# Reordering the steps of windowed attention in a two-layer decoder on one core

## The chip, the core and the metric

The kernel runs on one core of a Trainium2 chip. The metric is device time in microseconds (us) from launch to the last output; the lower the better. The core has five engines that run their own instruction streams and wait for each other through semaphores: TensorE (PE, matmuls; its weight loads are shown as PEld), VectorE (DVE), ScalarE (ACT), GpSimd (POOL) and SyncE (SP, which here only starts DMA transfers).

## The reference

A decoder trunk of two layers over 512 tokens with a model width of 1024, in float32. Layer 0 is a gated position mixer, a gated MLP with a short convolution, and a gated embedding. After it one shared key/value projection is made. Layer 1 is windowed attention over those keys and values, then the same MLP and embedding. The change is in the attention, whose core is:

```python
q = (xn @ w_q).reshape(B, nb, BLOCK, N_KV_HEADS, GQA_GROUP, HEAD_DIM)      # 4 blocks of 128, 4 groups of 4 heads
scores = jnp.einsum('bnikgd,bnjkd->bnkgij', q, kblk) * (HEAD_DIM ** -0.5)  # keys: previous and current block
scores = scores - slopes[:, :, None, None] * dist                          # ALiBi
scores = jnp.where(valid, scores, -jnp.inf)                                # window of 128, causal
m = jnp.maximum(jnp.max(scores, axis=-1, keepdims=True), sink)
e = jnp.exp(scores - m)
probs = e / (jnp.sum(e, axis=-1, keepdims=True) + jnp.exp(sink - m))
out = jnp.einsum('bnkgij,bnjkd->bnikgd', probs, vblk)
return out.reshape(B, S, N_Q_HEADS * HEAD_DIM) @ w_o
```

## The kernel before

**Products.** Every large product is made from float32 operands that are split in two parts, a high one (`wh`, `oh`, `n11h`, ...) and a low one (`wl`, `ol`, `n11l`, ...): three matmuls of 128 x 512 for each 128 rows of contraction (`mm3`, lines 212 to 214). Weights arrive by DMA in units of 512 KB (`wraw`, `load`); `pump` splits a unit, the high part on ACT (L185), the low part on DVE (L186). PE is in use for nearly the whole time.

**Attention in 16 steps.** A step is a pair of a key/value group g and a block n of 128 queries, g outer. For step i these pieces exist:

- `scores(i)` (L731): eight matmuls on PE into the tile `sc`, of which one buffer exists.
- `logits(i)` (L744, L745, L747, L750): DVE selects the window, scales and adds the ALiBi term, and takes the minimum `low` (the logits carry a minus sign). In a step with n = 0 L747 stands in L744's place, behind L745.
- `exps(i)` (L758): four exponentials on ACT, one for each head, each followed by a read-out of its sum into `sm`.
- `inverse(i)` (L763): the reciprocal of the four sums on DVE. `weights(i)` (L768): their product with the exponentials on POOL, in the tile `prs`.
- `turn(i)` (L775): four transposes on PE into `tr`. `turned_hi(i)` (L790, ACT) and `turned_lo(i)` (L795, DVE) split them into a high and a low part (`ph` and `pl` or `pp`), and `masks(i)` (L802, POOL) makes the masked copies `pm` for the difference of two value blocks.
- `mix(i)` (L816): the value product, four matmuls (two in a step with n = 0) into `pv`, of which one buffer exists. `low_rows(i)` (L822, ACT) copies its lower half to `pb`; `outputs(i)` adds the halves in two instructions on DVE (L834), after which `pv` is free, and makes the high part `oh` on ACT (L838); `output_lows(i)` makes the low part `ol` on POOL (L844).

**What runs beside it.** PE would be idle while a step goes through the other engines. So each step also has five entries of the list `work` (seven in the first), each of three matmuls: 48 entries for the queries of the later groups (`project`), then entries of the output projection (`merge`, tiles `o4`, `o5`, ...). `fill(i, a, b)` emits a step's entries a to b. When a query tile is complete, `queries` splits it (high part L274 on ACT, low part L275 on DVE) and sends the parts to their places by four DMAs; when an output tile is complete, DVE adds it to `h` (L865). Both are put in `held` and emitted by `settle()`.

**What sets the order.** Inside the block `in_order(...)` the order in which the code calls these pieces is the order on PE, DVE, ACT and POOL: each instruction follows the one before it on its engine. The loop of a step calls, in this order (step i >= 3):

```python
o = scores(i); weights(i - 1)
pairs = outputs(i - 3, *done.pop(i - 3)); logits(i, o); output_lows(pairs, nc.gpsimd)
pump(...); fill(i, 0, 3); tr = turn(i - 1); sinks(i + 1)
exps(i, (0, 1)); turned_hi(i - 1, tr); exps(i, (2, 3)); masks(...); turned_lo(i - 1, tr)
fill(i, 3, 4); settle(); pv = mix(i - 2); fill(i, 4, None)
inverse(i); done[i - 2] = pv, low_rows(i - 2, pv)
```

So a block's two sums (L834) are made one step after its value product, ahead of the next step's logits; the reciprocal stands at the end of the step, behind a query tile's split; and POOL's product of the probabilities opens the following step.

Of the kernel before, what the change touches and what calls it, by code (L numbers as in the profile page):

```python
# [52 lines left out]
def tile_yoco(ctx: ExitStack, tc: tile.TileContext, t, out: bass.AP, out_b: bass.AP):  # L53
    nc = tc.nc
# [36 lines left out]
    units = []  # L91
# [63 lines left out]
    def load(upto, queue=nc.sync):  # L155
        while state["raw"] < min(upto, len(units)):
            j = state["raw"]
            a, m, _ = units[j]
            tags = state["tags"]
            r = wp.tile([P, UNIT], F32, tag=f"r{tags[state['turn'] % len(tags)]}", bufs=1, name=f"wraw{j}")  # L160
            state["turn"] += 1
            if len(a.shape) == 4:
                for c in range(2):
                    queue.dma_start(r[:, :m].rearrange("p (k c n) -> p k c n", c=2, n=256)[:, :, c], a[:, :, c])
            else:
                queue.dma_start(r[:, :m], a)
            raws[j] = r
            state["raw"] += 1

    def pump(upto):  # L170
        while state["unit"] < min(upto, state["cap"]):
            u = state["unit"]
            _, n, own = units[u]
            load(u + 1)
            if own:
                pool, *tags = own
                wh, wl = (pool.tile([P, n], F32R, tag=tg, name=f"own{u}_{tg}") for tg in tags)
            else:
                wh = wp.tile([P, UNIT], F32R, tag="wh", bufs=WBUFS, name=f"wh{u}")
                wl = wp.tile([P, UNIT], F32R, tag="wl", bufs=WBUFS, name=f"wl{u}")  # L180
            src = raws.pop(u)[:, :n]
            if u == 0:
                nc.vector.tensor_copy(wh[:, :n], src)
            else:
                nc.scalar.copy(wh[:, :n], src)  # L185
            nc.vector.tensor_sub(wl[:, :n], src, wh[:, :n].bitcast(F32))  # L186
            ready[u] = (wh, wl, n)
            state["unit"] += 1
# [565 lines left out]
    def exps(i, es):  # L754

        pr, low, sm = live[i]
        for e in es:
            nc.scalar.activation(pr[:, e, :], pr[:, e, :], AF.Exp, bias=low[:, e : e + 1], scale=-1.0,  # L758
                                 accum_out=sm[:, e : e + 1])

    def inverse(i):

        nc.vector.reciprocal(live[i][2], live[i][2])  # L763

    def weights(i):

        pr, low, sm = live[i]
        nc.gpsimd.tensor_mul(pr[:, :, :P], pr[:, :, :P], sm.unsqueeze(2).to_broadcast([P, GQ, P]))  # L768
# [36 lines left out]
    def mix(i):  # L805

        g, n = steps[i]
        ph, pl, mh, ml = live.pop(i)
        cur = vt[n // 2][:, n % 2, g, :]
        terms = [(cur, ph), (cur, pl)]  # L810
        if n:
            dif = vd[:, n - 1, g, :]
            terms = [(cur, ph), (dif, mh), (cur, pl), (dif, ml)]
        ps = psum(f"pv{i}", "pv")
        for a, (lhs, rhs) in enumerate(terms):
            nc.tensor.matmul(ps, lhs, rhs, start=a == 0, stop=a == len(terms) - 1)  # L816
        return ps

    def low_rows(i, ps):

        b = tp.tile([P, S], F32, tag="rstd", name=f"pb{i}")
        nc.scalar.copy(b[:HD, :], ps[HD:, :])  # L822
        return b

    def outputs(i, ps, b):

        g, n = steps[i]
        if n == 0:
            for m in (2 * g, 2 * g + 1):
                o2.append([ap.tile([P, S], F32R, tag=f"a{x}{m}", name=f"o{x}{m}") for x in "hl"])  # L830
        x, y = (a.rearrange("p (b e t) -> p b e t", b=2, e=2) for a in (ps, b))
        of = y[:, :, 0, :]
        for e in range(2):
            nc.vector.tensor_add(of[sides[e]], x[:HD, :, e, :], y[:HD, :, e, :])  # L834
        cols = slice(n * P, (n + 1) * P)
        pairs = [(of[:, a, :], *(x[:, cols] for x in o2[2 * g + a])) for a in range(2)]
        for src, oh, ol in pairs:
            nc.scalar.copy(oh, src)  # L838
        return pairs

    def output_lows(pairs, eng):

        for src, oh, ol in pairs:
            eng.tensor_sub(ol, src, oh.bitcast(F32))  # L844
# [2 lines left out]
    held = []  # L847
    work = [(project, u) for u in range(48)]
    part = lambda m, k: (merge, m, k, k + 1, k == 0, k == 3 and m > 3)
    work += [part(m, k) for m, k in ((4, 0), (4, 1), (5, 0), (5, 1), (4, 2), (4, 3), (5, 2), (5, 3))]  # L850
    work += [part(m, k) for m in (6, 7, 0, 1, 2, 3) for k in range(4)]
    work += [part(0, 4), part(1, 4)]
    beside = [work[:7]] + [work[5 * i + 2 : 5 * i + 7] for i in range(1, last)]
    assert 5 * last + 2 == len(work)
# [2 lines left out]
    def fill(i, a, b):  # L857

        for f, *args in beside[i][a:b]:
            f(*args)  # L860

    def settle():

        for f, *args in held:
            f(*args)  # L865
        held.clear()
# [5 lines left out]
    with in_order(*engines):  # L872
        for i in range(last):
            o = scores(i)
            if i >= 1:
                weights(i - 1)
            if i >= 3:
                pairs = outputs(i - 3, *done.pop(i - 3))
            logits(i, o)
            if i >= 3:  # L880
                output_lows(pairs, nc.gpsimd)
            if i == 0:
                values(3)
            if i in pumped:
                pump(state["unit"] + 1)
            fill(i, 0, 3)
            if i:
                tr = turn(i - 1)
            if i + 1 < last:
                sinks(i + 1)  # L890
            exps(i, (0, 1))
            if i:
                turned_hi(i - 1, tr)
            exps(i, (2, 3))
            if i:
                masks(i - 1, (0,))
                turned_lo(i - 1, tr)
                masks(i - 1, (1,))
            fill(i, 3, 4)
            settle()  # L900
            if i >= 2:
                pv = mix(i - 2)
            fill(i, 4, None)
            inverse(i)
            if i % NC == NC - 1 and i + 1 < last:
                nc.vector.tensor_scalar_mul(alibi, alibi, slope(GQ - 1))
            if i >= 2:
                done[i - 2] = pv, low_rows(i - 2, pv)
            load(min(state["unit"] + 2, held_back))
        settle()  # L910
        weights(last - 1)
        output_lows(outputs(last - 3, *done.pop(last - 3)), nc.gpsimd)
        for m in (0, 1):
            merge(m, 5, 6, False, False)
        pv = mix(last - 2)
        done[last - 2] = pv, low_rows(last - 2, pv)
        merge(2, 4, 6, False, False)
        tr = turn(last - 1)
        turned_hi(last - 1, tr)
        masks(last - 1, (0,))  # L920
        turned_lo(last - 1, tr)
        masks(last - 1, (1,))
        output_lows(outputs(last - 2, *done.pop(last - 2)), nc.gpsimd)
    two = psum2("o4")
    merge(3, 4, 6, False, False)
    merge(4, 4, 6, True, False, two[:, 0])
# [219 lines left out]
```

## Time and profile before

| what | value |
|---|---|
| time, median of 3 runs | 1150.45 us (1149.15 to 1151.38) |
| the profiled execution, its own time | 1150.4 us |
| its span, first to last instruction | 1148.7 us |
| PE busy / DVE busy / ACT busy / POOL busy | 1125.6 / 734.6 / 509.8 / 136.0 us |
| mean granted TensorE clock | 0.996 |
| attention's 16 steps, first scores to last value product | from 590.8 us to about 703 us |

Busy time counts an instruction's whole duration; a matmul of 128 x 512 is shown with 389 ns, while the next one starts some 230 ns later, since they are pipelined. So an idle time of PE in the profile begins when the last matmul has ended by that model, and the distance between two starts is the better measure of what a wait costs.

### The profile page before, as it was taken

How to read it: one execution, taken by the hardware profiler on the slowest of the kernel's cores; microseconds unless marked ns; L12 is line 12 of the kernel's file. 1: busy time of each engine (PE TensorE's matmuls, PEld its weight loads, DVE VectorE, ACT ScalarE, POOL GpSimd, SP SyncE). 2: the span in 40 equal slices, each digit the busy share in tenths (PEclk: the TensorE clock that was granted, in tenths of full speed). 3: DMA queues.
4: the chain of work that ended last, by engine and by line, in shares of the span. 5: the costliest groups of instructions: out<-in, count | busy, mean ns of one | idle time of the engine just before them, and what ended most of it. 6: DMA issues, size and time to landing. Idle time of an engine off the chain costs nothing.

```text
span 1148.7 us, 13690 instructions
## 1 busy us (share of the span) xinstructions
PE 1125.6 (98%) x5248; PEld 938.3 (82%) x5248; DVE 734.6 (64%) x983; ACT 509.8 (44%) x808; POOL 136.0 (12%) x169
## 2 busy tenths in 40 slices
PE   9999999999999999999999899999999999999996
PEld 7888888888888888888897687888888888888895
DVE  7356477763676367557867776687735774577656
ACT  6534344431343244445646666554422442344532
POOL 2100310000000000022224444200000000000232
PEclk9999999999999999999999999999999999999998
DMA  9322222322322333233053314433323323332202
GB/s 319 123 80 86 98 94 91 110 94 90 110 82 83 110 113 99 83 110 110 19 147 110 110 56 147 147 110 92 110 82 102 95 71 110 110 97 85 79 15 74
DMA packets 44690, 116.48 MB, mean 101 GB/s; under 512 B 4936, under 2 KB 16848, under 8 KB 44624
## 3 DMA queue, kind: packets, MB, share of 16 engines
q1 hardware_dynamic: 43504, 114.42, 31.3%
q10 hardware_dynamic: 1120, 1.18, 0.3%
q8 instruction: 41, 0.67, 0.2%
q14 instruction: 25, 0.20, 0.1%
HBM read 108.24 MB, written 2.11 MB: 96 GB/s over the span
## 4 chain that ended last, share of the span: by engine, by line
PE 88%; DVE 5%; ACT 3%; issue 1%; POOL 1%; DMA 0%; SPq 0%; POOLq 0%; DVEq 0%; ACTq 0%
PE up L212 14%; PE up L213 14%; PE up L214 14%; PE d L212 8%; PE d L213 8%; PE d L214 8%; PE gate L212 2%; PE gate L213 2%; PE gate L214 2%; ACT prs L758 2%; PE u L214 1%; PE u L212 1%; PE u L213 1%; PE v L224 1%; PE v L223 1%; PE v L225 1%
## 5 line engine op out<-in xcount | busy, mean ns | idle before, releaser
L186 DVE TENSOR_TENSOR wl<-wraw,wh 128x1024 fp32r<-128x1024 f32 (+2 forms) x197 | 237.2, 1205 | 123.5 <-ACT wh L185 122.8
L185 ACT CAST wh<-wraw 128x1024 fp32r<-128x1024 f32 (+1 forms) x196 | 202.1, 1032 | 233.3 <-PE d L213 135.8
L212 PE MATMUL up<-nf00h,wh 128*128 128x512 f32 x352 | 137.1, 390 | 0.0
L212 PE MATMUL up<-nf10h,wh 128*128 128x512 f32 x352 | 137.0, 389 | 0.0
L214 PE MATMUL up<-nf00h,wl 128*128 128x512 f32 x352 | 137.0, 389 | 0.0
L214 PE MATMUL up<-nf10h,wl 128*128 128x512 f32 x352 | 136.9, 389 | 0.0
L213 PE MATMUL up<-nf00l,wh 128*128 128x512 f32 x352 | 136.9, 389 | 0.0
L212 PE MATMUL d<-ah,wh 128*128 128x512 f32 x352 | 136.9, 389 | 0.0
L213 PE MATMUL d<-al,wh 128*128 128x512 f32 x352 | 136.9, 389 | 0.0
L214 PE MATMUL d<-ah,wl 128*128 128x512 f32 x352 | 136.9, 389 | 0.0
L213 PE MATMUL up<-nf10l,wh 128*128 128x512 f32 x352 | 136.9, 389 | 0.0
L399 ACT ACTIVATE c<-hs,vec 128x512 f32<-128x512 f32 x88 | 71.7, 815 | 89.0 <-DVE hs L395 88.0
L400 DVE SCALAR_TENSOR_TENSOR c<-hs,vec,c 128x511 f32<-128x511 f32 x88 | 65.9, 749 | 37.4 <-ACT c L399 37.2
L373 DVE TENSOR_TENSOR h<-h,d 128x512 f32<-128x512 f32 x56 | 38.4, 686 | 69.0 <-PE d L214 69.0
L274 ACT CAST ah<-a 128x512 fp32r<-128x512 f32 x44 | 27.4, 622 | 113.5 <-DVE a L405 113.5
L214 PEld LDWEIGHTS up<-nf00h,wl 128*128 128x128 f32 x352 | 66.1, 188 | 13.8
L212 PEld LDWEIGHTS up<-nf10h,wh 128*128 128x128 f32 x352 | 66.1, 188 | 13.8
L214 PEld LDWEIGHTS d<-ah,wl 128*128 128x128 f32 x352 | 66.1, 188 | 13.8
L212 PEld LDWEIGHTS d<-ah,wh 128*128 128x128 f32 x352 | 66.1, 188 | 13.7
L213 PEld LDWEIGHTS up<-nf10l,wh 128*128 128x128 f32 x352 | 66.1, 188 | 13.7
L213 PEld LDWEIGHTS d<-al,wh 128*128 128x128 f32 x352 | 66.1, 188 | 13.6
L213 PEld LDWEIGHTS up<-nf00l,wh 128*128 128x128 f32 x352 | 66.1, 188 | 13.6
(316 smaller groups left out, 2028.6 us busy)
## 6 DMA issues: line engine op xcount, KB each, us to landing
wraw<-in_w_up SPq DMA_DIRECT2D x88, 512.0 KB, 3.5
wraw<-in_w_down SPq DMA_DIRECT2D x32, 512.0 KB, 3.6
wraw<-in_w_down SPq DMA_DIRECT2D x16, 384.0 KB, 3.2
wraw<-in_w_u SPq DMA_DIRECT2D x8, 512.0 KB, 6.7
wraw<-in_w_out SPq DMA_DIRECT2D x8, 512.0 KB, 3.5
wraw<-in_w_gate SPq DMA_DIRECT2D x8, 512.0 KB, 3.6
wraw<-in_w_q SPq DMA_DIRECT2D x8, 512.0 KB, 3.5
wraw<-in_w_o SPq DMA_DIRECT2D x8, 512.0 KB, 3.4
```

Of the source, the lines that this page charges most:

```text
L185: nc.scalar.copy(wh[:, :n], src)
L186: nc.vector.tensor_sub(wl[:, :n], src, wh[:, :n].bitcast(F32))
L212: nc.tensor.matmul(ps, wh[:, a:b], xh, start=st, stop=False)
L213: nc.tensor.matmul(ps, wh[:, a:b], xl, start=False, stop=False)
L214: nc.tensor.matmul(ps, wl[:, a:b], xh, start=False, stop=en)
L223: nc.tensor.matmul(ps, xh[:, s], wh[:, a:b], start=st, stop=False)
L224: nc.tensor.matmul(ps, xl[:, s], wh[:, a:b], start=False, stop=False)
L274: nc.scalar.copy(hi, src)
L373: nc.vector.tensor_add(h[m], h[m], ps)
L399: nc.scalar.activation(c, hs, AF.Identity, bias=v("conv_b", l * 2 * NJ + col), scale=cw[2])
L400: nc.vector.scalar_tensor_tensor(c[:, 1:], hs[:, : S - 1], cw[1], c[:, 1:], op0=ALU.mult, op1=ALU.add)
L758: nc.scalar.activation(pr[:, e, :], pr[:, e, :], AF.Exp, bias=low[:, e : e + 1], scale=-1.0, accum_out=sm[:, e : e + 1])
```

## The change

The number and kind of the instructions stay the same on every engine. The change puts attention's pieces in another order:

- `mix(i - 2)` moves from the step's end to right behind `scores(i)`, followed by its `low_rows`.
- `outputs(i - 2)`, with the two sums on DVE, is made in the same step, behind the logits' minimum, the first exponential and the low part of the turned probabilities. Before, it was made at the head of the next step.
- `inverse(i)` follows right behind these sums, ahead of the query tiles' splits and the additions to `h` of `settle()`, and POOL's `weights(i)` follows it in the same step.
- One exponential stands ahead of `turned_hi` on ACT instead of two; one entry of work stands ahead of the transposes on PE instead of three, three follow them, and the fifth closes the step.
- `pump` is cut in two, so that a unit's high part (ACT) stands ahead of the step's exponentials and its low part (DVE) behind them.
- The list of work puts the first two entries of output tile 6 ahead of the last two of tiles 4 and 5.

```diff
-    def pump(upto):
-        while state["unit"] < min(upto, state["cap"]):
-            u = state["unit"]
-            _, n, own = units[u]
-            load(u + 1)
+    half_done = {}
+
+    def pump_hi(u):
+
+        _, n, own = units[u]
+        load(u + 1)
+        if u not in half_done:
             if own:
...
                 nc.scalar.copy(wh[:, :n], src)
+            half_done[u] = wh, wl, n, src
+        return True
+
+    def pump(upto):
+        while state["unit"] < min(upto, state["cap"]):
+            u = state["unit"]
+            pump_hi(u)
+            wh, wl, n, src = half_done.pop(u)
             nc.vector.tensor_sub(wl[:, :n], src, wh[:, :n].bitcast(F32))
...
-    work += [part(m, k) for m, k in ((4, 0), (4, 1), (5, 0), (5, 1), (4, 2), (4, 3), (5, 2), (5, 3))]
-    work += [part(m, k) for m in (6, 7, 0, 1, 2, 3) for k in range(4)]
+    work += [part(m, k) for m, k in ((4, 0), (4, 1), (5, 0), (5, 1), (6, 0), (6, 1), (4, 2), (4, 3),
+                                             (5, 2), (5, 3), (6, 2), (6, 3))]
+    work += [part(m, k) for m in (7, 0, 1, 2, 3) for k in range(4)]
...
             o = scores(i)
-            if i >= 1:
-                weights(i - 1)
-            if i >= 3:
-                pairs = outputs(i - 3, *done.pop(i - 3))
             logits(i, o)
-            if i >= 3:
-                output_lows(pairs, nc.gpsimd)
+            cast = i and i in pumped and pump_hi(state["unit"])
+            if i >= 2:
+                pv = mix(i - 2)
+                low = low_rows(i - 2, pv)
             if i == 0:
                 values(3)
-            if i in pumped:
-                pump(state["unit"] + 1)
-            fill(i, 0, 3)
+            fill(i, 0, 1)
             if i:
                 tr = turn(i - 1)
             if i + 1 < last:
                 sinks(i + 1)
-            exps(i, (0, 1))
+            exps(i, (0,))
             if i:
                 turned_hi(i - 1, tr)
-            exps(i, (2, 3))
+            exps(i, (1, 2, 3))
+            if cast:
+                pump(state["unit"] + 1)
             if i:
                 masks(i - 1, (0,))
                 turned_lo(i - 1, tr)
                 masks(i - 1, (1,))
-            fill(i, 3, 4)
-            settle()
             if i >= 2:
-                pv = mix(i - 2)
-            fill(i, 4, None)
+                pairs = outputs(i - 2, pv, low)
             inverse(i)
+            weights(i)
+            if i >= 2:
+                output_lows(pairs, nc.gpsimd)
             if i % NC == NC - 1 and i + 1 < last:
                 nc.vector.tensor_scalar_mul(alibi, alibi, slope(GQ - 1))
-            if i >= 2:
-                done[i - 2] = pv, low_rows(i - 2, pv)
+            fill(i, 1, 4)
+            settle()
+            if i == 0:
+                pump(state["unit"] + 1)
+            fill(i, 4, None)
             load(min(state["unit"] + 2, held_back))
         settle()
-        weights(last - 1)
-        output_lows(outputs(last - 3, *done.pop(last - 3)), nc.gpsimd)
+        pv = mix(last - 2)
+        low = low_rows(last - 2, pv)
         for m in (0, 1):
             merge(m, 5, 6, False, False)
-        pv = mix(last - 2)
-        done[last - 2] = pv, low_rows(last - 2, pv)
+        pairs = outputs(last - 2, pv, low)
         merge(2, 4, 6, False, False)
         tr = turn(last - 1)
...
-        output_lows(outputs(last - 2, *done.pop(last - 2)), nc.gpsimd)
+        output_lows(pairs, nc.gpsimd)
```

**VectorE, from the logits of step 2 to the logits of step 3.** Names end in the step's number and a buffer number; `ql1_1` is the low part of a query tile, `pp1` that of the turned probabilities of step 1. Before:

```order
L750 TENSOR_REDUCE low2_4764<-prs_4587 128x4
L795 TENSOR_TENSOR pp1_4784<-tr1_4776,pp1_4784 128x512
L275 TENSOR_TENSOR ql1_1_4796<-q1_1_4712,qh1_1_4795 128x512
L763 RECIPROCAL sm2_4766<-sm2_4766 128x4
L834 TENSOR_TENSOR pb0_4813<-pv0_4805,pb0_4813 64x2x128 x2
L744 COPY_PREDICATED sc3_4815<-above_467,sc3_4815 128x4x128
L745 SCALAR_TENSOR_TENSOR prs_4587<-sc3_4815,rq_4382,alibi_4491 128x4x128
```

and with the change:

```order
L760 TENSOR_REDUCE low2_4764<-prs_4587 128x4
L805 TENSOR_TENSOR pp1_4782<-tr1_4775,pp1_4782 128x512
L844 TENSOR_TENSOR pb0_4770<-pv0_4767,pb0_4770 64x2x128 x2
L773 RECIPROCAL sm2_4766<-sm2_4766 128x4
L285 TENSOR_TENSOR ql1_1_4813<-q1_1_4728,qh1_1_4812 128x512
L754 COPY_PREDICATED sc3_4826<-above_467,sc3_4826 128x4x128
L755 SCALAR_TENSOR_TENSOR prs_4587<-sc3_4826,rq_4382,alibi_4491 128x4x128
```

The two sums and the reciprocal have moved ahead of the query tile's low part, which now stands alone between them and the next logits.

**TensorE, around the transposes of step 8 and the value product of step 7.** `o5_0` and `q3_1` are work that runs beside attention. Before, within step 9 and up to the scores of step 10:

```order
L775 MATMUL tr8_5275<-ident_131,prs_4587 128x128 x4
L212 MATMUL o5_0_5289<-oh0_4825,wh116_5043 128x512
L213 MATMUL o5_0_5289<-ol0_4826,wh116_5043 128x512
L214 MATMUL o5_0_5289<-oh0_4825,wl116_5044 128x512
L816 MATMUL pv7_5303<-pp7_5218,vt1_4489 128x512
L816 MATMUL pv7_5303<-pm7_5219,vd_4490 128x512
L816 MATMUL pv7_5303<-pp7_5218,vt1_4489 128x512
L816 MATMUL pv7_5303<-pm7_5219,vd_4490 128x512
L212 MATMUL o5_0_5289<-oh1_4827,wh116_5043 128x512
L213 MATMUL o5_0_5289<-ol1_4828,wh116_5043 128x512
L214 MATMUL o5_0_5289<-oh1_4827,wl116_5044 128x512
L731 MATMUL sc10_5316<-kh1_4288,q2_0_0_4945 128x256
```

and with the change, from the last scores of step 9:

```order
L741 MATMUL sc9_5247<-kl1_4290,q2_1_1_5100 128x256
L826 MATMUL pv7_5264<-pp7_5218,vt1_4489 128x512
L826 MATMUL pv7_5264<-pm7_5219,vd_4490 128x512
L826 MATMUL pv7_5264<-pp7_5218,vt1_4489 128x512
L826 MATMUL pv7_5264<-pm7_5219,vd_4490 128x512
L222 MATMUL q3_1_5168<-n11h7_3928,wh115_4908 128x512
L223 MATMUL q3_1_5168<-n11l7_3929,wh115_4908 128x512
L224 MATMUL q3_1_5168<-n11h7_3928,wl115_4909 128x512
L785 MATMUL tr8_5274<-ident_131,prs_4587 128x128 x4
```

The value product has moved ahead of the transposes, to the place behind the scores, with one entry of work between the two.

**TensorE, behind the scores of step 10.** `oh2` and `oh3` are outputs of the second group of heads, whose last block is step 7; `oh0` and `oh1` are of the first group. Before:

```order
L731 MATMUL sc10_5316<-kl1_4290,q2_1_1_5083 128x256
L212 MATMUL o4_0_5268<-oh2_5107,wh116_5043 128x512
L213 MATMUL o4_0_5268<-ol2_5108,wh116_5043 128x512
L214 MATMUL o4_0_5268<-oh2_5107,wl116_5044 128x512
L212 MATMUL o4_0_5268<-oh3_5109,wh116_5043 128x512
```

and with the change:

```order
L741 MATMUL sc10_5323<-kl1_4290,q2_1_1_5100 128x256
L826 MATMUL pv8_5340<-ph8_5281,vt0_4488 128x512
L826 MATMUL pv8_5340<-pl8_5282,vt0_4488 128x512
L222 MATMUL o6_0_5345<-oh0_4791,wh117_5122 128x512
L223 MATMUL o6_0_5345<-ol0_4792,wh117_5122 128x512
L224 MATMUL o6_0_5345<-oh0_4791,wl117_5123 128x512
L785 MATMUL tr9_5349<-ident_131,prs_4587 128x128 x4
L222 MATMUL o6_0_5345<-oh1_4793,wh117_5122 128x512
L223 MATMUL o6_0_5345<-ol1_4794,wh117_5122 128x512
L224 MATMUL o6_0_5345<-oh1_4793,wl117_5123 128x512
L222 MATMUL o4_0_5297<-oh2_5072,wh116_5043 128x512
```

The first matmul that reads the second group's outputs was the first one behind the scores; now it stands three items later, and those outputs are made one step earlier.

## The prediction

> **What bounds the kernel now.** I read the page's first rows, then PE's waits, then the granted clock around the longest wait, then the timelines of the engines there.
>
> ```profile
> span 1148.7 us, 13690 instructions
> PE 1125.6 (98%) x5248; PEld 938.3 (82%) x5248; DVE 734.6 (64%) x983; ACT 509.8 (44%) x808; POOL 136.0 (12%) x169
> ```
>
> PE has work for 98% of the span, and the change neither adds nor removes a matmul. It can only move the 23 us in which PE stands still, and what the clock costs. The list of PE's waits says how much of that lies in attention:
>
> ```profile
> PE tr L775 <- POOL prs L768: 4.2, 6, 1.3
> PE o L212 <- ACT oh L838: 2.9, 1, 2.9
> PE pv L816 <- DVE pb L834: 0.9, 1, 0.9
> ```
>
> (us in total, times, longest.) The transposes wait six times for POOL's product of the probabilities; the output projection waits once, for the second group's outputs; one value product of the tail waits for `pv` to be read out. That is 8.0 us of idle time. Idle time starts at a modelled end, so it understates what a wait costs:
>
> ```profile
> 636.90 0.39 PE L213 MATMUL q<-n11l,wh 128*128 128x512 f32 x1
> 637.13 0.39 PE L214 MATMUL q<-n11h,wl 128*128 128x512 f32 x1
> 638.84 0.66 PE L775 MATMUL tr<-ident,prs 128*128 128x128 f32 x4 [1.32 <-POOL prs L768]
> 648.26 0.28 PE L731 MATMUL sc<-kh,q 128*128 128x256 f32 x1
> 651.67 0.66 PE L775 MATMUL tr<-ident,prs 128*128 128x128 f32 x4 [0.24 <-POOL prs L768]
> 654.48 0.28 PE L731 MATMUL sc<-kh,q 128*128 128x256 f32 x1
> 655.31 0.28 PE L731 MATMUL sc<-kl,q 128*128 128x256 f32 x1
> 658.45 0.79 PE L212 MATMUL o<-oh,wh 128*128 128x512 f32 x1 [2.86 <-ACT oh L838]
> ```
>
> A matmul of 0.39 us is followed by the next after 0.23, so each wait costs 0.16 us more than its idle time. Eight waits: 8.0 + 8 x 0.16 = **9.3 us**. The longest one also costs clock (columns: stretch, its length, busy time of PE, PEld, DVE, ACT, POOL, granted clock, DMA):
>
> ```profile
> 657.00:658.00 1.00, 0.00 (x0) 0.00 (x0) 0.99 (x5) 0.07 (x1) 0.55 (x1) 1.00 0.72 260
> 658.00:659.00 1.00, 0.55 (x1) 0.31 (x2) 0.90 (x3) 0.90 (x3) 1.00 (x3) 0.54 0.79 193
> 659.00:660.00 1.00, 1.00 (x3) 0.81 (x3) 0.90 (x2) 0.55 (x1) 0.47 (x2) 0.50 0.90 215
> 660.00:661.00 1.00, 1.00 (x4) 0.80 (x3) 1.00 (x2) 0.70 (x4) 0.00 (x0) 0.50 0.21 49
> 661.00:662.00 1.00, 1.00 (x5) 0.81 (x4) 0.39 (x1) 0.18 (x2) 0.00 (x0) 0.76 0.00 0
> 630.00:640.00 10.00, 8.68 (x47) 7.08 (x46) 8.06 (x16) 7.05 (x20) 5.38 (x10) 1.00 0.33 95
> ```
>
> After a gap of 2.86 us the clock is granted at half for some 3.4 us, and PE loses 0.46 + 0.50 + 0.50 + 0.24 = **1.7 us**. After gaps of 1.3 us (last row) it stays at 1.00. So 11.0 us are at stake.
>
> Why PE waits there is seen in the other engines' timelines around step 9 (and, for one row, POOL's at 637.74, the product that PE's transposes of 638.84 wait for):
>
> ```profile
> 651.37 0.68 DVE L744 COPY_PREDICATED sc<-above,sc 128x512 f32<-128x512 uint32 x1
> 653.00 0.69 DVE L750 TENSOR_REDUCE low<-prs 128x4 f32<-128x516 f32 x1
> 653.61 1.22 DVE L186 TENSOR_TENSOR wl<-wraw,wh 128x1024 fp32r<-128x1024 f32 x1
> 653.73 0.40 ACT L758 ACTIVATE prs<-prs,low 128x129 f32<-128x129 f32 x1 [0.74 <-DVE low L750]
> 654.64 0.59 ACT L790 CAST ph<-tr 128x512 fp32r<-128x512 f32 x1
> 655.26 0.69 DVE L795 TENSOR_TENSOR pl<-tr,ph 128x512 fp32r<-128x512 f32 x1 [0.43 <-ACT ph L790]
> 655.90 0.57 ACT L274 CAST qh<-q 128x512 fp32r<-128x512 f32 x1
> 656.50 0.69 DVE L275 TENSOR_TENSOR ql<-q,qh 128x512 fp32r<-128x512 f32 x1 [0.56 <-ACT qh L274]
> 657.11 0.17 DVE L763 RECIPROCAL sm<-sm 128x4 f32<-128x4 f32 x1
> 657.20 0.82 DVE L834 TENSOR_TENSOR pb<-pv,pb 64x256 f32<-64x256 f32 x2
> 637.74 1.04 POOL L768 TENSOR_TENSOR prs<-prs,sm 128x512 f32<-128x512 f32 x1 [0.78 <-DVE sm L763]
> 657.45 1.04 POOL L768 TENSOR_TENSOR prs<-prs,sm 128x512 f32<-128x512 f32 x1 [4.52 <-DVE sm L763]
> 658.10 0.50 ACT L838 CAST oh<-pb 128x128 fp32r<-128x128 f32 x2 [1.02 <-DVE pb L834]
> ```
>
> The reciprocal (657.11) and the sums (657.20) stand behind the query tile's low part `ql`, which waited for its high part. POOL's product and the outputs `oh` follow from them, and PE waits for both. This is the order that the change undoes.
>
> **Part by part: what is removed.** *The wait for `oh`* (2.86 + 0.16 + 1.7 of clock): the outputs come a step earlier and their first reader three items later. One item, three matmuls, is 0.69, so the margin grows by a step (below 5.8) and about 2 us, against 3.0 missing: gone. *The six waits for POOL*: the reciprocal now starts 0.08 before the sums end (as it did before `ql`'s end, 657.19), POOL starts 0.34 after the reciprocal's start (657.11 to 657.45) and takes 1.04, and PE follows 0.06 behind its end (638.78 to 638.84): the transposes can start 1.36 after the sums' end. The value product, which needs that end too, and one item keep PE for 4 x 0.23 + 0.69 = 1.61 us, so no wait is left; in the three steps that follow an n = 0 block the product is two matmuls, 1.15 in all, and about 0.15 remains in some: **0.3**. *The wait in the tail*: its sums are also made earlier; I leave **0.2** of it.
>
> **What is added.** `pv` has one buffer. The value product of step i + 1 may start only when the sums of step i have read it out, and it now stands right behind the scores, where before a whole step lay between. So per step a chain must fit between two scores. Its length, from the end of the scores: window to minimum 651.37 to 653.69, 2.32; to the end of one exponential with its read-out 0.54; cast `ph` 0.62 and low part 0.72, each with 0.03 of hand-over; two sums 0.77; release of PE 0.06: **5.03 us**. PE's time from scores to scores is 654.48 - 648.26 = 6.22, less the one wait in it (0.24 + 0.16): 5.8. Less 0.16, since the product can be issued before the last scores have ended: **0.6 us of slack**. The split's low part (1.22) fits beside the exponential and the cast (1.16) within 0.1, as part of that slack.
>
> The slack holds only if DVE is free when the scores end. In six steps (1, 2, 4, 6, 7, 9) `settle()` puts a query tile's split right behind the sums, and the next logits queue behind it. It waits for ACT: 0.08 to the casts `oh`, 0.41, then `qh` 0.57, 0.03, then `ql` 0.61 until DVE is free: logits start 1.7 us after the sums' end. If the sums ended 0.6 before the scores, the next product is late by 1.7 - 0.6 - 0.6 = about 0.4; if they already ended late, as in the second of two neighbouring steps (2 and 7), by 1.05. Four x 0.4 + two x 1.05 = **3.7**. Additions to `h` also stand there:
>
> ```profile
> 663.93 1.27 DVE L865 TENSOR_TENSOR h<-h,o 128x512 f32<-128x512 f32 x2
> 671.13 0.40 DVE L906 TENSOR_SCALAR alibi<-alibi 128x512 f32<-128x512 f32 x1
> ```
>
> Step 11 has two of them and the change of ALiBi's slope, 0.09 + 0.32 + 1.19 = 1.6, as late as a query tile: **0.5**. Steps with a single one (0.7) stay within the slack.
>
> **Costed at nothing.** The cast ahead of the exponentials on ACT (1.04) fits into the wait for `low` that ACT has anyway (0.74 idle behind the cast in the quoted row at 653.73); without that cover each exponential would come later and the chain with it. Behind it stands the copy of `pv`'s lower half (0.6), which ends some 1.9 after the scores, ahead of `low` at 2.3. The query tiles' DMAs go out in the step in which they did; a tile's last parts are needed a step (5.8) or more later, and land in 2.4:
>
> ```profile
> q<-qh SPq DMA_DIRECT2D x16, 128.0 KB, 2.4
> ```
>
> The earlier tile 6 changes nothing but the order of equal items.
>
> **The sum.** Added 0.3 + 0.2 + 3.7 + 0.5 = 4.7. Bounds: 1.5, if the query splits find DVE idle, to 9.3, if the new waits grow as long as the old. I take 4.7, which the rows give. Net -11.0 + 4.7 = -6.3 us. From the profiled execution's 1150.4 that is **1144.1 us**; that execution and the median (1150.45) are the same within 0.1.
>
> The Trainium skill, TensorE: Matmul & The Clock Gate, Part 1, has the clock fall after at least one idle window of about 3.4 us. Here 2.86 us sufficed, so the measurement decides, and I take the 1.7 us as belonging to this wait. By the page a gap of that length alone would not do it, and the sum would be 1145.8.
>
> **The rivals.** *The new wait replaces the old ones in full.* The eight links of the chain may each take longer than I count; from 0.6 us more on, every one of the 13 products of steps 3 to 15 waits. At 0.35 us each that adds 4.6: 1148.7, hardly a gain. For it: the chain is 5.0 of 5.8. Against: all its terms come from one step and are short of nothing that I see. *The clock falls again (the slower side).* The new waits come in neighbouring steps (3 and 4, 8 and 9), and somewhere between gaps of 1.3 and 2.86 us the clock gives way. If the six query steps each cross that point, six dips of 1.7 make 1144.1 + 10.2 = 1154.3. It decides from waits of some 2 us on; mine are 1.05 at most, and the stretch from 630 to 640, with a wait of 1.32, has 1.00. The page on TensorE, A second HAM failure mode, in the Trainium skill, says that frequent small idle times between groups of matmuls make the clock oscillate, which speaks for this rival; six gaps of up to 1.3 us here did not. *The dip comes back elsewhere*, not tied to this gap: 1144.1 + 1.7 = 1145.8. *The query split costs less*: if the products wait only in the two neighbouring pairs and the sums otherwise end early, the added part is 1.5 and the time 1140.9.
>
> **How the numbers follow.** Forecast 65% (its own range 1142.0 to 1146.5), replaced wait 10%, clock 5%, the dip elsewhere 7%, cheaper split 13%. The range of 8 in 10, 1140.8 to 1148.0, leaves out the clock rival, most of the replaced wait and a part of the cheapest case. What a measurement can tell from no change is about 0.2%, 2.3 us. Faster by more: forecast, dip elsewhere, cheaper split and a little of the replaced wait, 0.86; within: the rest of that, 0.09; slower: 0.05.
>
> **What would show it.** PE's list of waits should no longer hold `tr` for POOL above 0.5 us in all, nor `o` for `oh`; it should hold `pv` for DVE's sums, six to nine times, 3 to 5 us in total, none over 1.2, in the steps behind query splits. The clock should be 1.00 throughout attention, and DVE's timeline should show the logits starting behind `ql`. I am wrong if `tr` still waits for POOL, if `pv` waits in nearly every step, or if the clock dips.

## The result, and the profile after

| | before | after |
|---|---|---|
| time, median | 1150.68 us (1149.15 to 1151.38) | 1144.81 us (1144.61 to 1144.89) |
| ratio | | 0.995, 95% interval 0.9935 to 0.9964 |
| span of the profiled execution | 1148.7 us | 1142.9 us |
| mean granted clock in it | 0.996 | 0.997 |

The changed kernel is 5.9 us faster; 1144.1 was forecast. The page's first rows (span; then each engine's busy time, share and count of instructions):

```profile
span 1142.9 us, 13705 instructions
PE 1124.6 (98%) x5248; PEld 937.9 (82%) x5248; DVE 736.5 (64%) x983; ACT 509.7 (45%) x808; POOL 136.3 (12%) x169
```

PE does the same 5248 matmuls; its work has not shrunk, its waits have. (The two totals differ by 15 instructions that are not counted as busy.) The list of PE's waits after (what waited, line, for what; us in total, times, longest):

```profile
PE pv L826 <- DVE pb L844: 2.9, 6, 0.7
PE ht L1006 <- DVE z L968: 1.8, 1, 1.8
PE idle L264 <- DVE minus_half L266: 1.5, 1, 1.5
PE sc L741 <- DMA q<-ql: 0.5, 1, 0.5
```

The six waits of the transposes for POOL and the one for the outputs are gone. In their place the value product `pv` waits six times for the sums, which must read out its one buffer, and the scores of step 4 wait once for the second query tile's transfer. With 0.16 a wait for the modelled ends, that is 2.9 + 6 x 0.16 + 0.5 + 0.16 = 4.5 us left over, where 4.7 was forecast. (The waits for `z` and `minus_half` lie outside attention and stand in the profile of before as well.) The clock over attention, as a row of the view by stretches (stretch, length, busy time of PE, PEld, DVE, ACT, POOL, granted clock, DMA share, GB/s), first of before, then of after:

```profile
590.00:720.00 130.00, 121.89 (x649) 101.45 (x648) 94.48 (x156) 81.01 (x234) 54.10 (x90) 0.99 0.35 107
```

```profile
590.00:720.00 130.00, 126.32 (x674) 106.19 (x673) 99.96 (x161) 85.51 (x240) 57.38 (x92) 1.00 0.37 112
```

In the same 130 us PE is busy 4.4 us longer, and the dip is gone: the clock is 1.00 in each of the 13 stretches of 10 us. VectorE's timeline around two steps of the changed kernel shows what the new waits come from (start, duration, engine, line, operation):

```profile
619.97 0.69 DVE L760 TENSOR_REDUCE low<-prs 128x4 f32<-128x516 f32 x1
...
622.44 0.84 DVE L844 TENSOR_TENSOR pb<-pv,pb 64x256 f32<-64x256 f32 x2
623.31 0.18 DVE L773 RECIPROCAL sm<-sm 128x4 f32<-128x4 f32 x1
624.38 0.69 DVE L285 TENSOR_TENSOR ql<-q,qh 128x512 fp32r<-128x512 f32 x1 [0.90 <-ACT qh L284]
624.99 0.69 DVE L754 COPY_PREDICATED sc<-above,sc 128x512 f32<-128x512 uint32 x1
...
626.63 0.69 DVE L760 TENSOR_REDUCE low<-prs 128x4 f32<-128x516 f32 x1
628.50 0.69 DVE L805 TENSOR_TENSOR pl<-tr,ph 128x512 fp32r<-128x512 f32 x1 [1.17 <-ACT ph L800]
629.11 0.84 DVE L844 TENSOR_TENSOR pb<-pv,pb 64x256 f32<-64x256 f32 x2
...
630.07 0.67 DVE L754 COPY_PREDICATED sc<-above,sc 128x512 f32<-128x512 uint32 x1
...
631.70 0.69 DVE L760 TENSOR_REDUCE low<-prs 128x4 f32<-128x516 f32 x1
```

The sums end at 623.28, the logits start at 624.99, behind `ql`: 1.71 us, as forecast. The prediction did not use a second reading of such rows, and it turned out to be the more useful one: **the distance from one minimum to the next**. Here it is 626.63 - 619.97 = 6.66 us in the step with a query split (step 4), and 631.70 - 626.63 = 5.07 in the one without (step 5). The same three minima before:

```profile
620.71 0.69 DVE L750 TENSOR_REDUCE low<-prs 128x4 f32<-128x516 f32 x1
...
627.28 0.69 DVE L750 TENSOR_REDUCE low<-prs 128x4 f32<-128x516 f32 x1
629.53 0.69 DVE L795 TENSOR_TENSOR pl<-tr,ph 128x512 fp32r<-128x512 f32 x1 [1.56 <-ACT ph L790]
630.30 0.18 DVE L763 RECIPROCAL sm<-sm 128x4 f32<-128x4 f32 x1
630.91 0.85 DVE L834 TENSOR_TENSOR pb<-pv,pb 64x256 f32<-64x256 f32 x2 [0.43 <-ACT pb L822]
631.68 0.68 DVE L744 COPY_PREDICATED sc<-above,sc 128x512 f32<-128x512 uint32 x1
...
633.32 0.69 DVE L750 TENSOR_REDUCE low<-prs 128x4 f32<-128x516 f32 x1
```

6.57 and 6.04 us. VectorE's idle time inside these steps ended on ScalarE, never on PE's scores. So a loop through VectorE and ScalarE (minimum, exponentials, `ph`, `pl`, split, sums, next logits, minimum) needed more than PE's own 5.8 us in these steps of before, and PE waited wherever the loop reached it. In these two steps the change took 1.0 us out of the one without a split and nothing out of the one with it (steps 8 and 9 are alike). The split stays between the sums and the next logits, so its steps stay long.

The rows say where the 1.0 lies. The low part `pl` starts 1.87 us behind the minimum instead of 2.25: one exponential instead of two stands ahead of its high part on ScalarE. The sums start 0.61 behind the low part instead of 1.38: neither the reciprocal nor ScalarE's copy `pb`, which stood behind all four exponentials, comes between. From the sums to the logits it is 0.96 instead of 0.77, because the reciprocal stands there now. No run tests these moves one by one. Over all the steps, from the first minimum to the last, the distance falls from 97.4 to 91.3 us; 2.4 of that lie in step 10, with the wait for the outputs.

### The profile page after: what moved, and what is told of

It is laid out like the page before. It is cut to its first block, busy times and chain, and to the rows that moved or that the text cites. A ratio compares the mean times of both kernels' runs of the same rounds, so it can differ in the third digit from the quotient of the medians.

```text
span 1142.9 us, 13705 instructions
## 1 busy us (share of the span) xinstructions
PE 1124.6 (98%) x5248; PEld 937.9 (82%) x5248; DVE 736.5 (64%) x983; ACT 509.7 (45%) x808; POOL 136.3 (12%) x169
## 4 chain that ended last, share of the span: by engine, by line
PE 90%; DVE 5%; ACT 2%; issue 1%; POOL 1%; DMA 0%; SPq 0%; POOLq 0%; DVEq 0%; ACTq 0%
PE up L224 14%; PE up L223 14%; PE up L222 14%; PE d L223 8%; PE d L224 8%; PE d L222 8%; PE gate L222 2%; PE gate L224 2%; PE gate L223 2%; PE u L224 1%; PE u L222 1%; PE u L223 1%; PE v L234 1%; PE v L233 1%; PE v L235 1%
```

## The experiments

Each kernel ran beside the kernel before on the same chip, in five rounds, on three chips; before was 1150.76, 1150.89 and 1150.72 us there.

**Which part removes the wait for the outputs?** The changed kernel with the old list of work:

```diff
-    work += [... (5, 0), (5, 1), (6, 0), (6, 1), (4, 2), (4, 3), (5, 2), (5, 3), (6, 2), (6, 3))]
+    work += [... (5, 0), (5, 1), (4, 2), (4, 3), (5, 2), (5, 3))]
```

> The changed kernel with the old list of work, so that the first reader of the second group's outputs stands again right behind step 10's scores and value product. Theory M (the outputs are made one step earlier, and that alone removes PE's wait for oh): 1144.8 us within 0.6, no wait of o for oh over 0.3 us, clock 1.00 in attention. Rival W (the new list of work removed it): the wait of 2.9 us and the dip of the clock (1.7 us) come back, 1149.4 us.

Measured: 1144.28 us (1143.93 to 1144.62), ratio 0.9943 (0.993 to 0.9957), and no wait for `oh`. The earlier outputs suffice by themselves: M holds and W is out. In the changed kernel the new order of the list is worth nothing; the half microsecond by which this kernel is faster is not clear of the two intervals. The same list in the kernel before:

> The kernel before with the new list of work alone. Two items (1.4 us) now stand between step 10's scores and the first reader of the second group's outputs, against a wait of 3.0. Theory M: a wait of about 1.6 us is left, and with a gap that short the clock stays at 1.00: 1150.5 - 1.4 - 1.7 = 1147.4 us. Rival P (the dip of the clock is not tied to that gap): half clock for 3.4 us is seen in attention all the same, 1149.1 us. Rival W (the list is what the change gains by): 1145 to 1146 us.

Measured: 1149.49 us (1148.78 to 1149.98), ratio 0.9989 (0.998 to 0.9997). PE's waits in it:

```profile
PE tr L775 <- POOL prs L768: 5.0, 8, 1.3
...
PE o L212 <- ACT oh L838: 1.5, 1, 1.5
PE o L212 <- DVE pp L795: 0.8, 1, 0.8
```

The 2.9 us became 1.5, and behind this shorter gap the profile shows the clock at 1.00. Counted from the first scores matmul of a step to that of the next, PE gains 2.5 us in step 10 (9.88 before, 7.36 here). It hands back 0.6 in each of steps 12 and 13 (5.72 and 5.76 become 6.30 and 6.34), where the transposes now wait for POOL: with this list two additions to `h` instead of one stand ahead of the reciprocal on VectorE in step 11. (In the tail an `o` waits 0.8, in place of the 0.9 of a value product.) The expectation, which only took the one wait away, was 2 us too low; the profiled execution, the fastest of the eleven, took 1148.78. Rival P named 1149.1 and is out for that execution, which shows no dip. For the others only the mean clock was kept, 0.995 to 0.997, so there it stays open.

**Is the early reciprocal, with POOL's product, needed?** The changed kernel with these put back to the step's end:

```diff
-            inverse(i)
-            weights(i)
-            if i >= 2:
-                output_lows(pairs, nc.gpsimd)
             if i % NC == NC - 1 and i + 1 < last:
...
             fill(i, 4, None)
+            inverse(i)
+            weights(i)
+            if i >= 2:
+                output_lows(pairs, nc.gpsimd)
             load(min(state["unit"] + 2, held_back))
```

> The changed kernel with reciprocal, POOL's product and the outputs' low parts put back to the end of the step, behind the query tiles' splits and the additions to h. Theory M (the reciprocal's place is what removed PE's waits for POOL): the transposes wait again for POOL in the six steps with a query split and in step 11, about 1.2 us each, 8 us in all; PE then comes later to the value products, so their waits for the sums (4.6 us by distance of starts) go: net +3.5, 1148.3 us. Rival S (the sums' place alone did it): 1144.8 us and no wait of tr.

Measured: 1147.49 us (1147.01 to 1147.81), ratio 0.997 (0.9959 to 0.9982). The transposes wait again, and the value products no longer do (the list of waits has no row for them):

```profile
PE tr L785 <- POOL prs L778: 6.7, 8, 1.2
```

So in the changed kernel the early place of the reciprocal, with POOL's product and the outputs' low parts behind it, is worth 2.7 us. Is the reciprocal enough by itself? The kernel before, with the reciprocal alone moved ahead of the split:

```diff
+            inverse(i)
             fill(i, 3, 4)
             settle()
...
             fill(i, 4, None)
-            inverse(i)
```

> The kernel before with one line moved: the reciprocal of a step stands ahead of the query tile's split; POOL's product is still issued behind the next scores, the sums still come a step later. Theory M (the places of the value product, its sums and the settling make the gain together): POOL's product in a step with masks stands behind the second mask, which waits for the low part, so an earlier reciprocal moves it by little, and the next logits still stand behind the split; PE's waits of the transposes for POOL stay at 3 to 4.5 us in all (4.2 before), the wait of the output projection for the outputs stays at 2.5 to 3.0, and the time is 1150.0 (1148.8 to 1150.8). Rival R (the reciprocal behind the split was the fault by itself): the transposes' waits fall below 1 us, and the time is 1145.5.

Measured: 1152.16 us (1150.84 to 1153.46), ratio 1.0011 (1.0002 to 1.002): *slower*. R is out, and M missed the sign (the transposes wait 5.3 us in all, where it had 3 to 4.5). POOL's product does start earlier, but the minima keep their distances (6.52 and 6.04 in steps 4 and 5): the reciprocal takes 0.1 us of VectorE, and nothing in the loop waits for it. What made it slower shows most in step 11 (7.42 us from minimum to minimum instead of 6.41), VectorE's and POOL's timelines of this kernel, then of before:

```profile
671.75 1.24 DVE L906 TENSOR_SCALAR alibi<-alibi 128x512 f32<-128x512 f32 x1
...
671.67 1.04 POOL L768 TENSOR_TENSOR prs<-prs,sm 128x512 f32<-128x512 f32 x1
```

```profile
671.13 0.40 DVE L906 TENSOR_SCALAR alibi<-alibi 128x512 f32<-128x512 f32 x1
...
671.37 1.06 POOL L768 TENSOR_TENSOR prs<-prs,sm 128x512 f32<-128x512 f32 x1
```

The change of ALiBi's slope takes 1.24 us when POOL's product has just begun, 0.40 when it comes first. To test this, it was moved ahead of the reciprocal in that kernel:

```diff
+            if i % NC == NC - 1 and i + 1 < last:
+                nc.vector.tensor_scalar_mul(alibi, alibi, slope(GQ - 1))
             inverse(i)
```

> The kernel with the reciprocal alone moved (1152.2 on this work's chips), with the change of ALiBi's slope moved ahead of the reciprocal, so that it never runs beside POOL's product of the same step. Theory C (VectorE's scaling of ALiBi took 0.83 and 1.24 us in that kernel instead of 0.40 because POOL's product was running, and all that follows on VectorE came later): it takes 0.40 again where POOL is not in its product, and the time falls by 0.8 to 1.3, to 1150.9 to 1151.4. Rival: the loss came from elsewhere (the waits of the transposes and of the output projection that end later), and the time stays at 1151.8 to 1152.5.

Measured: 1150.21 us (1148.32 to 1150.6), ratio 0.9993 (0.9984 to 1.0001), 1.95 less than without. The scaling takes 0.42 in all three places (in the kernel with the reciprocal alone 0.80, 0.83 and 1.24):

```profile
670.25 0.42 DVE L900 TENSOR_SCALAR alibi<-alibi 128x512 f32<-128x512 f32 x1
```

Theory C holds, with more gain than the 0.8 to 1.3 that it expected; the three rows explain 1.6 of the 1.95. In the first of the three POOL was still in a mask, not in its product. The kernel before has 0.80, 0.40 and 0.40 in these places, so 0.3 of the half microsecond by which this kernel is below it is the scaling's as well. What is left for the reciprocal's place alone is some 0.2 us, which the interval does not tell from nothing.

**Is it the split ahead of the next logits that the new waits come from?** The changed kernel with the settling one place later:

```diff
             logits(i, o)
+            settle()
...
             fill(i, 1, 4)
-            settle()
```

> The changed kernel with settle (query splits and additions to h) moved behind the next step's logits. Theory M (the new wait of pv for the sums comes from a query split that stands between the sums and the next logits): those waits fall from 2.9 us of idle time to under 1.2; the query tiles' DMAs go out some 3 us later, so step 4's scores wait longer for theirs, 0.5 to 1.2 us: net -3, 1142 us. Rival L (the chain from scores to sums is too long by itself): the waits stay at 2.5 us or more, 1144.5 to 1145.5 us.

Measured: **1141.02 us** (1140.96 to 1141.23), ratio 0.9915 (0.9901 to 0.9928), the fastest kernel of this work: 3.8 us below the changed one. PE's waits, then VectorE in the same steps 4 and 5:

```profile
PE pv L826 <- DVE pb L844: 0.6, 2, 0.3
...
PE sc L741 <- DMA q<-ql: 0.3, 1, 0.3
```

```profile
618.96 0.69 DVE L760 TENSOR_REDUCE low<-prs 128x4 f32<-128x516 f32 x1
...
623.02 0.70 DVE L754 COPY_PREDICATED sc<-above,sc 128x512 f32<-128x512 uint32 x1 [0.54 <-PE sc L741]
...
624.68 0.69 DVE L760 TENSOR_REDUCE low<-prs 128x4 f32<-128x516 f32 x1
625.29 0.68 DVE L285 TENSOR_TENSOR ql<-q,qh 128x512 fp32r<-128x512 f32 x1
...
630.47 0.69 DVE L760 TENSOR_REDUCE low<-prs 128x4 f32<-128x516 f32 x1
```

Now VectorE waits for PE's scores (0.54), the distances are 5.72 and 5.79, and `ql` no longer waits for `qh`, which ScalarE has made (by 623.34) before the minimum starts. In these steps PE sets the pace. The chain can also be cut at the other end, by putting the sums directly behind the minimum, ahead of both low parts (`sums` is the two additions on VectorE, taken out of `outputs`):

```diff
             exps(i, (1, 2, 3))
+            if i >= 2:
+                sums(i - 2, pv, low)
             if cast:
                 pump(state["unit"] + 1)
```

> The changed kernel with the two sums of a value product directly behind the minimum on VectorE, ahead of the weights' and the transposes' low parts. Theory M (a value product that waits does so because the sums read out the single buffer at the end of a chain behind late logits): the sums leave the chain of casts and low parts, some 1.3 us earlier, so the product's waits fall from 4.6 us to 1 to 2, and the time to 1141.8 (1140.8 to 1143.0). Rival K (the products wait for something else, or the low parts that now come later make the same wait elsewhere): the time stays at 1144.0 to 1145.5, with waits of 4 us or more on the products or the transposes.

Measured: 1142.93 us (1142.5 to 1143.23), ratio 0.9931 (0.9919 to 0.9944). No value product waits for the sums any more; two wait for POOL's mask of a low part that now comes later, and the scores wait longer for the query tile:

```profile
PE sc L741 <- DMA q<-ql: 1.0, 2, 0.8
...
PE pv L826 <- POOL pm L812: 0.4, 2, 0.3
```

M names the right buffer, but the time is at the upper end of its range: a part of the gain is taken by what the early sums make late. Two more kernels tried to go on from the best one. First, the settling of step 2 alone put back to that step's end, for the second query tile:

> As the kernel in which the settling stands behind the next step's logits (1141.0 on this chip), but in step 2 it stays at the step's end, so that the second query tile is split and sent a little earlier. Theory D (the scores of step 4 wait for that tile's transfers): the scores of step 4 no longer wait (they lost 0.26 us there, counted from start to start), the product of step 4 waits up to 0.7 instead, and the time is 1140.6 (1140.2 to 1141.1). Rival: what the one wait gives, the other takes in full, 1141.0 to 1141.4. The two differ by less than the interval may show; the trace's row of the scores of step 4 decides.

Measured: 1141.39 us (1141.14 to 1141.76), ratio 0.9918 (0.9904 to 0.9931); the scores of step 4 still wait:

```profile
616.59 0.30 PE L741 MATMUL sc<-kh,q 128*128 128x128 f32 x1 [0.34 <-DMA q<-ql]
617.25 0.47 PE L826 MATMUL pv<-ph,vt 128*128 128x512 f32 x1 [0.25 <-DVE pb L844]
```

D's forecast is out: the earlier split brings the tile hardly sooner, since SyncE ends the last of its four issues at 614.70 instead of 614.82 (one of them takes 1.15), and the product waits as well. Then that kernel with the sums first:

> The changed kernel with both: the sums directly behind the minimum, and the settling behind the next step's logits except in step 2. If the two gains rest on the same wait (theory M), they do not add up: the products' waits fall to 0.5 to 1.5 us and the time is 1140.4 (1139.8 to 1141.2). If they were two separate costs, 1144.8 - 3.0 - 3.8 = 1138.0.

Measured: 1142.55 us (1142.39 to 1143.02), ratio 0.9929 (0.9916 to 0.9941). The gains do not add up, as M says, but M's time is missed by 2 us: it is even 1.5 behind the best kernel, with products waiting for the later masks (`PE pv L826 <- POOL pm L812` with 1.1 us in five waits). Both cures act on one wait, and the masks and low parts that the early sums delay cost more than M allowed.

**How much of the gain is the loop alone?** If VectorE's loop set the pace already before, then the settling one place later must help the *old* kernel too, with its product, sums and reciprocal where they were:

```diff
             logits(i, o)
+            settle()
...
             fill(i, 3, 4)
-            settle()
```

> The kernel before with one line moved: the settling (query tiles' splits, held additions to h) stands behind the next step's logits; value product, sums, reciprocal and list as before. Theory L (in both kernels a loop through VectorE and ScalarE, minimum to minimum, sets the pace in steps with a query split: 6.5 to 6.6 us, against 6.04 in other steps and 5.8 of TensorE's own work): these distances fall to 6.1 or less, the transposes' waits for POOL from 4.2 to 1 to 2 us, the wait for the outputs stays at 2 to 3, the second query tile's transfers are waited for in step 4, and the time is 1147.2 (1146.0 to 1148.5). Rival P (the product and the sums being issued a step late is what held TensorE, as the prediction told it): the transposes still wait 3 us or more and the time is 1149.5 to 1150.8.

Measured: 1146.5 us (1145.42 to 1147.9), ratio 0.9963 (0.9951 to 0.9975). PE's waits, and two steps of VectorE:

```profile
PE o L212 <- ACT oh L838: 2.3, 1, 2.3
...
PE pv L816 <- DVE pb L834: 1.4, 1, 1.4
PE sc L731 <- DMA q<-ql: 1.1, 2, 0.8
PE tr L775 <- POOL prs L768: 0.3, 1, 0.3
```

```profile
619.57 0.69 DVE L750 TENSOR_REDUCE low<-prs 128x4 f32<-128x516 f32 x1
625.61 0.69 DVE L750 TENSOR_REDUCE low<-prs 128x4 f32<-128x516 f32 x1
626.22 0.68 DVE L275 TENSOR_TENSOR ql<-q,qh 128x512 fp32r<-128x512 f32 x1
631.52 0.69 DVE L750 TENSOR_REDUCE low<-prs 128x4 f32<-128x516 f32 x1
```

6.04 and 5.91 us instead of 6.57 and 6.04; the transposes' waits for POOL fall from 4.2 to 0.3, though POOL's product is still issued behind the next scores. L is right and P is out. The wait for the outputs stays, with its dip of the clock (0.64, 0.50, 0.50 and 0.66 in the four stretches of 1 us from 655), and the scores of step 4 now wait 1.1 us for the second query tile, as L expected. With the new list of work added:

> The kernel before with two of its parts: the settling behind the next step's logits, and the new list of work. Theory L: the gains add up, since the one shortens VectorE's loop and the other shortens the wait of the output projection: 1146.0 (1145.0 to 1147.2), that is most of the changed kernel's gain with the value product and its sums still where they were. Rival P: 1148.5 to 1149.5, as with the new list alone.

Measured: 1144.69 us (1144.17 to 1144.96), ratio 0.9947 (0.9935 to 0.9958). These two edits to the kernel before reach what the whole change reaches (1144.81). The time is below L's range (1145.0 to 1147.2): the wait for the outputs falls to 0.9 us and the dip goes with it, and since the additions to `h` stand behind the next logits now, step 11 stays at 6.20 us from minimum to minimum, where the new list alone had 7.02.

The distances from minimum to minimum, worked out from VectorE's rows as above (us; steps 4 and 9 have a query split, 5 and 8 have none):

| kernel | step 4 | 5 | 8 | 9 | time |
|---|---|---|---|---|---|
| before | 6.57 | 6.04 | 6.04 | 6.57 | 1150.7 |
| before, reciprocal alone | 6.52 | 6.04 | 6.04 | 6.51 | 1152.2 |
| before, settling later | 6.04 | 5.91 | 5.90 | 6.04 | 1146.5 |
| after, reciprocal and product late | 6.74 | 5.77 | 5.73 | 6.75 | 1147.5 |
| after | 6.66 | 5.07 | 5.07 | 6.67 | 1144.8 |
| after, sums first | 6.15 | 5.41 | 5.45 | 6.15 | 1142.9 |
| after, settling later | 5.72 | 5.79 | 5.72 | 5.77 | 1141.0 |

A pair of steps takes 12.6 us before, 11.7 after and 11.5 in the best kernel, against 11.6 by PE's own two steps of 5.8. These pairs hold only a part of what the last kernel gains over the changed one. More of it lies where two query splits are neighbours: the minima of steps 1 and 4 are 18.0 us apart after and 16.9 in the best kernel, those of steps 6 and 8 13.4 and 11.6.

## Why the prediction was right, point by point

- *What is removed (11.0 us).* Right: no wait of the transposes or for the outputs is left, and the clock is 1.00 throughout attention. The margin for the outputs is ample even without the new list, as the kernel with the old one shows. (Two entries of work, not three, stand ahead of their first reader; with the value product and the transposes, which stand there too, it is still some 2 us.)
- *The cause.* Half right. "The reciprocal and the sums stand behind `ql`" is what the trace shows, but the reciprocal alone, moved, gave nothing, and the split alone, moved, gave 4.2 us. The late reciprocal was where PE met the delay; the delay was the split's place in VectorE's queue ahead of the next logits. The change did not alter that place; it shortened the rest of the loop, so that the steps without a split make up for those with one. The prediction worked out that chain for the changed kernel only (5.03 of 5.8) and not for the kernel before, where the same reading gives 6.04 and 6.57.
- *Left over: 0.3 for the transposes, 0.2 in the tail.* The first is 0; the product of the tail does not appear among the six waits. So neither of these two terms came.
- *Six query splits (3.7) and step 11 (0.5).* Right in place and in sum: 2.9 + 6 x 0.16 = 3.9 against 4.2, and taking the splits from ahead of the logits gave 3.8 back. Five waits stand behind query splits and one, of 0.62, behind step 11; behind the split of step 2 the scores of step 4 waited for the tile instead. The shares were less uneven than 0.4 and 1.05: the six waits are 0.15 to 0.68 of idle time. (By the prediction's own rounded terms, 1.7 less 0.6 and 0.6 is 0.5, and 1.7 less 0.6 is 1.1, so its 3.7 would be 4.2.) "None over 1.2" and "six to nine times" hold; the 2.9 us of idle time lie just below "3 to 5".
- *Costed at nothing: the query tiles' transfers.* Wrong in one place. Step 4 waits 0.5 + 0.16 us for the second tile. The prediction gave a tile "a step (5.8) or more" against 2.4 of landing and left out SyncE's own time to issue the four transfers of a tile, and that a tile is split late in its step. SyncE after, then the scores that waited:

```profile
612.05 0.46 SPq L646 DMA_DIRECT2D q<-qh  x1
612.78 1.30 SPq L647 DMA_DIRECT2D q<-ql  x1
614.12 0.60 SPq L646 DMA_DIRECT2D q<-qh  x1
614.76 0.60 SPq L647 DMA_DIRECT2D q<-ql  x1
```

```profile
617.27 0.30 PE L741 MATMUL sc<-kh,q 128*128 128x128 f32 x1 [0.51 <-DMA q<-ql]
```

  From the first issue to the last transfer's landing it is some 5.2 us (612.05 to 617.2), nearly the whole step. Before, the second issue took 0.46, the four began at 611.20, and the scores of step 4 did not wait. Why it takes 1.30 after was not found.
- *The rivals.* The replaced wait did not come: 4.5 us is left of 11.0. The clock did not fall. "The query split costs less" (1140.9) is not what the changed kernel does, but the time is close to what the kernel with the moved split reaches (1141.0), by another way than the rival's.
- *The sum.* -6.3 forecast, -5.9 measured. Removed less left over, 11.0 - 4.5, would be 6.5; where the 0.7 between that and the spans' 5.8 lies was not traced. That 4.5 is left over where 4.7 was forecast is in part luck: the 0.5 for the transposes and the tail did not come, and 0.66 for the query tile, costed at nothing, did.

## What to carry to other kernels

When an engine waits many times for a short while, don't price each wait by itself: take the distance between the same instruction of successive steps on every engine, and the engine whose own chain fills that distance, without waiting for the one that is meant to be the bound, sets the pace. Look for work in that chain that nobody needs soon (here a query tile's split, with a wait for another engine in the middle of it) and put it behind the instruction that the next round starts from. Here one moved line gave 4.2 us to the old kernel and 3.8 to the new one, the reordering of everything else 5.9.

## What the runs showed of the hardware

**VectorE and POOL hinder each other.** The scaling of ALiBi (128 x 512, float32, 0.40 us at its shortest) took 1.24 us when it started 0.08 behind POOL's product, and ended 0.28 after it. The two other long ones of that kernel (0.80 and 0.83) also ended 0.29 after the POOL instruction that had started ahead of them. With the scaling first, POOL's mask, which started 0.15 behind it, took 0.76 instead of 0.64. The Trainium skill, SBUF — State Buffer, section "SBUF: two separate sides", describes an exclusive lock on a pair of ports that GpSimd shares with some VectorE instructions (those in a two-port mode or with two inputs in SBUF), held for the whole instruction, by which the one that comes second is blocked. The rows agree with the lock; in which mode the scaling runs, no row here shows. The kernel with the scaling ahead got 1.95 us back. In a list of an engine's waits this does not show: the blocked instruction only looks longer.

**The clock fell behind gaps of 2.3 us and more.** In the four kept profiles in which PE stands idle for 2.33 to 2.86 us at the wait for the outputs (the kernel before, and before with the reciprocal alone, with the scaling ahead of it, and with the settling later), the granted clock is 0.50 soon after the gap, for some 3.4 us. Behind the gap of 1.48 (the new list in the kernel before), and behind the 1.8 ahead of `ht` in the kernels before and after, it stays at 1.00. These are single profiles. Of the kernel before, 4 of the 48 runs beside the experiments have a mean clock of 0.997 or 0.998 and 1148.9 to 1149.8 us; the others, with 0.992 to 0.996, have mostly 1150 to 1151.6. That fits a dip of 1.7 us in most runs and none in a few, but no profile of one of the few was kept. With the gap shortened to 1.48, 11 runs still spread from 0.995 to 0.998, so the clock may fall in some of these as well. The mean is not a clean measure, since it holds the program's end, where PE has no work left and the clock falls 3.1 us (after) to 5.3 us (the new list in the kernel before) behind the last matmul. The Trainium skill, TensorE: Matmul & The Clock Gate, Part 1, asks for at least one idle window of about 3.4 us before the clock falls; none of the gaps in attention is that long, so here the measurement decides.
